# A step of a hybrid decoder: TensorE's work in the attention takes the order of the program text

## The chip, the core and the metric

The kernel runs on one core of a Trainium2 chip. A core has five engines that run side by side: TensorE (matrix products, PE in the rows), VectorE (DVE), ScalarE (ACT), GpSimd (POOL) and SyncE (SP), which here issues most transfers. Each takes its own list of instructions in the order in which it stands in the program and waits on semaphores for the others. The metric is the device time of one execution in microseconds (us); the kernel before takes 1497.58 us (median of 3 runs, 1497.58 to 1500.13).

## The reference

One step of a small decoder: a state-space layer (S5) and then an attention layer, for a prompt of 1024 tokens and for 8 samples of 8 new tokens, which have 2048 past tokens each in a paged cache. Both layers have their own weights; keys and values come once, from the stream after the S5 layer. The change touches only the attention, whose weights are "stick-breaking":

```
z = q·k * scale + bias                       # per head, strictly causal mask
log_fail = where(mask, log_sigmoid(-z), 0)
later = reverse_cumsum(log_fail) - log_fail  # all keys between this one and the query
A = where(mask, exp(log_sigmoid(z) + later), 0)
o = A @ v
x + rms_norm((o * silu(g)) @ w_out, g_post)  # g: the gate, the second half of h @ w_in
```

There are 16 heads of 64 columns, so 8 head pairs. Samples run the same on 16 pages of 128 past keys and on their own new ones.

## The kernel before, in words

The attention's main loop (in `attention`, `for slot in range(-LAG, n_row)`) runs over 128 rows. A row is one head with one block of 128 queries; pairs of heads follow each other, in a pair four groups of 256 queries (qp = 0 to 3, with growing numbers of keys), in a group two heads with two blocks each. The tiles psb, psa, psqk and psmm are PSUM banks (3, 2, 2 and 1 of them).

Three kinds of work for TensorE are woven together in the text of a slot:

- The prompt. `prompt.scores` of the row three slots ahead (LAG = 3): products psqk<-ks,qh and psqk<-ks,ql (L1139, L1140); then ScalarE forms two sigmoids (F, S; L1141, L1142), VectorE scans F (L1146, L1148), VectorE or GpSimd multiplies S by F (L1149). `prompt.turn` of the row itself: S is transposed in 128-column blocks (psb<-cst,S, L1164) and taken out masked (L1168). After each fourth row `prompt.values` of the group before: psb<-at,vr (L1182), 64 columns of the array, the two heads of the pair side by side, and then og (L1186). Keys of a pair are cut in a high and a low part (ks, L1103 on ScalarE and L1104 on VectorE); its values stand in one buffer, vr (L1107, `bufs=1`), filled again for each pair.
- The gates: `gate(ct)`, 72 full-array products per pair (psmm<-x,whi_g and wlo_g, L147 to L149) in nine pieces.
- The samples: `stream(...)`, a generator of steps: two pages of keys (kp, L990) for scores, two pages of values (vp, L949), transposes (L1004). L990 and L949 use 32 columns of the array, four instructions for its four quarters after each other. Pages come through three buffers.

`pump(slot, part)` is called twice in a slot and gives the gates and samples so many pieces that they end evenly over the pairs.

The text so written is not the order in which an engine's instructions stand. The program is built with a planner (`schedule_with_timeline_sim=True`): it goes through the instructions with a model of their durations and puts on each engine what it thinks ready first, the text's order only deciding between those that are ready. So a score product, a transpose or a piece of a gate can stand between the four quarters of a page group, or between the two heads of a value product. At run time TensorE keeps to the order that the planner wrote.

Of the kernel before, what the change touches and what calls it, by code (L numbers as in the profile page):

```python
# [144 lines left out]
def mm3(nc, ps, sh, sl, mh, ml, k, n):  # L145

    nc.tensor.matmul(ps, sh, mh, start=(k == 0), stop=False)  # L147
    nc.tensor.matmul(ps, sh, ml, start=False, stop=False)  # L148
    nc.tensor.matmul(ps, sl, mh, start=False, stop=(k == n - 1))  # L149


def kernel_body(tc, io, upto=9):
    nc = tc.nc
    with ExitStack() as root:
# [34 lines left out]
        with tc.tile_pool(name="w", bufs=2, reuse_waits="tile") as wp:  # L189
# [5 lines left out]
            with tc.tile_pool(name="y2s", bufs=1, side="right", reuse_waits="tile") as ysp:  # L195
                y2, ys = s5_glu(tc, nc, io, wp, x1, ysp, bank, zs_d, s2, *parts)
                (x1h, x1l), wq0 = s5_out(tc, nc, io, wp, x1, bank, ident, y2, ys, ysp, x1_d, gw, gains)
        attention(tc, nc, io, bank, left, gws, gw, gains, ident, x1h, x1l, wq0, x1_d, q_d, o_d)


# [405 lines left out]
def attention(tc, nc, io, bank, x1s, gws, gw, gains, ident, x1h, x1l, wq0, x1_d, q_d, o_d):  # L606
    V, Q = nc.vector, nc.gpsimd
    with ExitStack() as st:
# [146 lines left out]
        def pump(slot, part):  # L755

            pi, r = divmod(slot, 16)
            frac = (pi + sum(SHARE[: r // 4]) + SHARE[r // 4] * ((r % 4) + part) / 4) / (KT - 1)
            for f in fills:
                while f[2] < min(1.0, frac) * f[1]:  # L760
                    next(f[0], None)
                    f[2] += 1
# [3 lines left out]
        def out_steps():  # L766
            for qp in range(3, -1, -1):
                while qp not in done:
                    yield
                for t in (2 * qp, 2 * qp + 1):  # L770
                    yield from first_half(t)

        for slot in range(-LAG, n_row):
            if slot + LAG < n_row:
                prompt.scores(*rows[slot + LAG])
            if slot < 0:
                for _ in range(9 // LAG + 1):
                    next(g0, None)
                continue
            def beside(part):  # L780
                if fin is None:
                    pump(slot, part)
                else:
                    for _ in range(2):
                        next(outs, None)

            beside(0.5)
            if slot % 4 == 0 and slot:
                pi, qp = groups[slot // 4 - 1]
                prompt.values(pi, qp, sgt[pi], None if pi < KT - 1 else fin)  # L790
                if fin and pi == KT - 1:
                    done.append(qp)
            if slot == n_row - 16:
                for f in fills:
                    for _ in f[0]:
                        pass
                sst.close()
                gws.close()
                x1s.close()
                fp = st.enter_context(tc.tile_pool(name="fin", bufs=1, side="right", reuse_waits="tile"))  # L800
                fin = [[fp.tile([128, SEQ], F32R, name=f"o{n}{k}") for k in range(KT)] for n in "hl"]
                fr = st.enter_context(tc.tile_pool(name="fin_r", bufs=1, side="right", reuse_waits="tile"))
                osg = fr.tile([128, KT, NTS], F32, name="osg")
                V.tensor_tensor(osg, osam.rearrange("p k s t -> p k (s t)"), sgs, op=ALU.mult)
                ps_s = [bank("a")]
                halves = [out_half(nc, fr, io["b_wout"], 0, osg, ps_s[0])]
                for k in range(KT - 1):
                    r = fr.tile([128, SEQ], F32, name=f"or{k}", tag="or", bufs=2)
                    nc.sync.dma_start(r, o_d[k])
                    nc.scalar.activation(fin[0][k], r, AF.Copy)  # L810
                    (V if k % 2 else Q).tensor_tensor(fin[1][k], r, fin[0][k], op=ALU.subtract)

                gp = []

                def gain(pool):
                    g = pool.tile([128, 512], F32, name=f"gpost_b{len(gp)}", bufs=1)
                    nc.sync.dma_start(g, io["b_gpost"][:, len(gp) * 512 : len(gp) * 512 + 512].to_broadcast([128, 512]))
                    gp.append(g)

                gain(fr)  # L820

                def gained(name, half, src, o, acc, n=128):

                    sq = fr.tile([128, 512], F32, name=f"sqo{half}_{name}", tag="wro", bufs=2)
                    nc.scalar.activation(sq[:n], src, AF.Square, accum_out=acc[:n])
                    V.tensor_tensor(o[:n], src, gp[half][:n], op=ALU.mult)

                def out_tile(t, half, o, acc):
                    ps = bank(next(free))
                    sl = slice(t * 128, t * 128 + 128)  # L830
                    wh, wl = halves[half]
                    for k in range(KT):
                        mm3(nc, ps, fin[0][k][:, sl], fin[1][k][:, sl], wh[k], wl[k], k, KT)
                        yield
                    gained(t, half, ps, o, acc)

                def out_sample(half, o, acc):
                    f = fr.tile([128, 512], F32, name=f"osum{half}", tag="wro", bufs=2)
                    nc.scalar.activation(f[:NTS], ps_s[half][NTS:], AF.Copy)
                    V.tensor_tensor(f[:NTS], ps_s[half][:NTS], f[:NTS], op=ALU.add)  # L840
                    gained("s", half, f[:NTS], o, acc, NTS)

                first = {}
                free = chain(("mm", "a", "a") * 2, cycle(("b", "qk", "a", "b", "mm", "qk", "a", "b")))

                def firsts(t):
                    s2 = fr.tile([128, 2], F32, name=f"s2_{t}", bufs=1)
                    f = fr.tile([128, 512], F32, name=f"oa{t}", bufs=1)
                    first[t] = f, s2
                    return f, s2[:, 0:1]  # L850

                def first_half(t):
                    yield from out_tile(t, 0, *firsts(t))

                f, acc = firsts(8)
                V.memset(first[8][1], 512.0)
                out_sample(0, f, acc)
                outs = out_steps()

            prompt.turn(*rows[slot])  # L860
            beside(1)
# [37 lines left out]
def out_half(nc, pool, src, half, osg, ps, bufs=2):  # L899


    wh, wl = [], []
    for k in range(KT):
        raw = pool.tile([128, 512], F32, name=f"wr_o{half}{k}", tag="wro", bufs=bufs)
        nc.sync.dma_start(raw, src[k * 128 : (k + 1) * 128, half * 512 : half * 512 + 512])
        rows = slice(k % 2 * NTS, k % 2 * NTS + NTS)
        nc.tensor.matmul(ps[rows], osg[:, k], raw, start=(k < 2), stop=(k > 5))
        h = pool.tile([128, 512], F32R, name=f"woh{half}{k}", bufs=1)
        l = pool.tile([128, 512], F32R, name=f"wol{half}{k}", bufs=1)
        nc.scalar.activation(h, raw, AF.Copy)  # L910
        nc.vector.tensor_tensor(l, raw, h, op=ALU.subtract)
        wh.append(h)
        wl.append(l)
    return wh, wl
# [485 lines left out]
```

## Time and profile before

| | |
|---|---|
| median of 3 runs | 1497.58 us |
| profiled execution, its own time | 1500.17 us |
| its span | 1498.4 us |
| TensorE busy | 1415.8 us (94%) |
| VectorE busy | 935.0 us (62%) |
| ScalarE, GpSimd busy | 718.2 us (48%), 493.7 us (33%) |
| attention loop, in the trace | 872 to 1430 us |

Shares over the whole span mix the S5 stages with the attention, which has other limits. A matrix product's end is modelled, and products overlap in the array: so the start of one to the start of the next tells its cost, not the duration beside it. In the trace each instruction of L949, L990, L961 and L1182 stands as two records (two passes of a 32-bit product), every other product of the loop as one.

### The profile page before, as it was taken

Reading aid. Unit: us, or ns where it says so; the run is one execution under the profiler, and the core shown is the slowest. Engines: PE = TensorE matmul, PEld = TensorE weight load, DVE = VectorE, ACT = ScalarE, POOL = GpSimd, SP = SyncE. Lnnn points to the kernel's source line nnn. Section 1 sums busy time; section 2 is a strip of 40 time slices with the busy share of each in tenths; the row PEclk is TensorE's granted clock in tenths of the full one; section 3 lists DMA queues with packets and bytes.
Section 4 is the critical chain, followed back from the end, with each engine's and each line's share of the span. In section 5 each row is a group of like instructions: output and inputs, shape, how many; then the busy total and the mean of one; then the engine's idle time right before and its main releaser. Section 6 shows DMA issues by size and latency. Waiting matters only on the chain.

```text
span 1498.4 us, 26819 instructions
## 1 busy us (share of the span) xinstructions
PE 1415.8 (94%) x9648; PEld 1145.8 (76%) x9648; DVE 935.0 (62%) x1506; ACT 718.2 (48%) x1424; POOL 493.7 (33%) x473
## 2 busy tenths in 40 slices
PE   4987988899999989999999999999998999998997
PEld 3987978899977889999988877666565665565766
DVE  6877887758755531110122149897888888789545
ACT  5233454454434433332333347676665766576321
POOL 6556565325412132222111012433323233334200
PEclk9999999999999999999999999999999999999999
DMA  5345556674134252232288755979878686754026
GB/s 197 103 129 139 140 126 163 145 251 145 58 106 132 91 224 91 85 123 100 103 314 298 255 201 192 339 284 326 295 257 289 250 308 219 268 190 139 11 82 213
DMA packets 129670, 276.41 MB, mean 184 GB/s; under 512 B 21633, under 2 KB 66562, under 8 KB 129538
## 3 DMA queue, kind: packets, MB, share of 16 engines
q1 hardware_dynamic: 127234, 268.41, 54.0%
q10 hardware_dynamic: 2304, 6.29, 1.3%
q8 instruction: 76, 1.25, 0.3%
q14 instruction: 56, 0.46, 0.1%
HBM read 224.55 MB, written 39.35 MB: 176 GB/s over the span
## 4 chain that ended last, share of the span: by engine, by line
PE 75%; DVE 9%; POOL 5%; DMA 4%; issue 3%; ACT 2%; SPq 1%; DVEq 0%; POOLq 0%; ACTq 0%
PE psmm L147 7%; PE psmm L149 7%; PE psmm L148 7%; PE psqk L147 6%; PE psqk L148 6%; PE psqk L149 6%; PE psa L949 5%; PE psb L1182 5%; PE psb L1164 4%; PE psa L990 4%; PE psqk L1139 3%; PE psqk L1140 2%; DMA cf<-cs 2%; PE psa L147 2%; PE psa L149 2%
## 5 line engine op out<-in xcount | busy, mean ns | idle before, releaser
L1120 POOL TENSOR_TENSOR ql<-q,qh 128x256 fp32r<-128x256 f32 x64 | 62.5, 977 | 285.6 <-ACT qh L1119 246.5
L1141 ACT ACTIVATE F<-psqk,bp 128x384 f32<-128x384 f32 (+2 forms) x192 | 111.3, 580 | 64.6 <-PE psqk L1140 49.2
L1146 DVE TENSOR_TENSOR_SCAN F<-F,maskb 128x256 f32<-128x256 f32 (+3 forms) x128 | 131.2, 1030 | 14.0 <-ACT F L1141 13.6
L1149 POOL TENSOR_TENSOR S<-S,F 128x255 f32<-128x255 f32 (+3 forms) x64 | 100.8, 1574 | 115.7 <-DVE F L1148 22.5
L1142 ACT ACTIVATE S<-psqk,bp 128x384 f32<-128x384 f32 (+2 forms) x192 | 111.4, 583 | 22.7 <-PE psb L1164 22.6
L1164 PE MATMUL psb<-cst,S 128*128 128x128 f32 x576 | 96.7, 285 | 4.4 <-DVE og L1186 3.8
L1164 PEld LDWEIGHTS psb<-cst,S 128*128 128x128 f32 x576 | 67.3, 143 | 35.1 <-issue 20.5
L1148 DVE TENSOR_TENSOR_SCAN F<-F 128x384 f32<-128x384 f32 (+1 forms) x64 | 78.9, 1233 | 20.4 <-ACT F L1141 19.8
L1182 PE MATMUL psb<-at,vr 128*64 128x256 f32 (+1 forms) x640 | 90.0, 369 | 1.2 <-DVE at L1168 1.2
L949 PE MATMUL psa<-vp,sat 128*32 128x256 f32 x1024 | 86.1, 388 | 0.1
L1139 PE MATMUL psqk<-ks,qh 128*128 128x384 f32 (+2 forms) x192 | 77.4, 404 | 6.9 <-DVE ks L1104 5.2
L990 PE MATMUL psa<-kp,qbd 128*32 128x256 f32 x1024 | 75.5, 389 | 0.5 <-PE psb L1164 0.5
L1182 PEld LDWEIGHTS psb<-at,vr 128*64 128x64 f32 x640 | 46.7, 137 | 36.6 <-issue 10.3
L1168 DVE TENSOR_TENSOR at<-psb,maskb 128x384 f32<-128x384 f32 (+3 forms) x128 | 60.3, 478 | 21.3 <-PE psb L1164 20.7
L147 PE MATMUL psmm<-xh,whi_u 128*128 128x408 f32 (+1 forms) x192 | 65.3, 341 | 3.7 <-ACT ut L278 3.1
L147 PE MATMUL psmm<-x,whi_g 128*128 128x408 f32 (+1 forms) x192 | 66.6, 347 | 1.1 <-DVE gt L739 1.1
L943 DVE TENSOR_TENSOR_SCAN sF<-sF 128x513 f32<-128x513 f32 x32 | 44.4, 1388 | 36.1 <-ACT sF L940 35.8
L1139 PEld LDWEIGHTS psqk<-ks,qh 128*128 128x128 f32 x192 | 37.0, 193 | 37.8 <-ACT S L1142 12.8
L1140 PE MATMUL psqk<-ks,ql 128*128 128x384 f32 (+2 forms) x192 | 65.8, 344 | 0.0
L148 PE MATMUL psmm<-xl,whi_u 128*128 128x408 f32 (+1 forms) x192 | 65.4, 341 | 0.0
L149 PE MATMUL psmm<-x,wlo_g 128*128 128x408 f32 (+1 forms) x192 | 64.9, 338 | 0.2 <-DVE wlo_g L141 0.2
L148 PE MATMUL psmm<-x,whi_g 128*128 128x408 f32 (+1 forms) x192 | 65.1, 339 | 0.0
(452 smaller groups left out, 4234.6 us busy)
## 6 DMA issues: line engine op xcount, KB each, us to landing
kp<-cache_kT SPq DMA_DIRECT2D x128, 512.0 KB, 6.0
vp<-cache_v SPq DMA_DIRECT2D x128, 512.0 KB, 5.7
cf<-cs SPq DMA_DIRECT2D x32, 256.0 KB, 5.4
q<-q_d SPq DMA_DIRECT2D x128, 64.0 KB, 4.6
u_d<-ut SPq DMA_DIRECT2D x8, 544.0 KB, 2.8
ug<-u_d SPq DMA_DIRECT2D x64, 68.0 KB, 2.9
y_d<-gt SPq DMA_DIRECT2D x64, 68.0 KB, 2.4
zs_d<-zt SPq DMA_DIRECT2D x8, 544.0 KB, 4.5
```

The lines of the kernel that those rows point to most:

```text
L147: nc.tensor.matmul(ps, sh, mh, start=(k == 0), stop=False)
L148: nc.tensor.matmul(ps, sh, ml, start=False, stop=False)
L149: nc.tensor.matmul(ps, sl, mh, start=False, stop=(k == n - 1))
L949: self.nc.tensor.matmul(po[32 * r : 32 * r + 32, 0:256], a[:, 32 * r : 32 * r + 32], rhs[:, r * 256 : (r + 1) * 256], start=start, stop=stop)
L990: nc.tensor.matmul(ps[32 * r : 32 * r + 32, half * 256 : half * 256 + 256], self.qbd[:, 2 * r + e, s, :], kt[:, :, 2 * r + e, :], start=(e ...
L1139: nc.tensor.matmul(ps[:, :m], qh[:, w], ks[:, c0 : c0 + m], start=True, stop=False)
L1141: nc.scalar.activation(F[:, c0 : c0 + m], ps[:, :m], AF.Sigmoid, bias=bp[:, 1, h : h + 1], scale=-0.125)
L1142: nc.scalar.activation(S[:, c0 : c0 + m], ps[:, :m], AF.Sigmoid, bias=bp[:, 0, h : h + 1], scale=0.125)
L1146: V.tensor_tensor_scan(fr, fr, self.maskb[:, 512 - m : 512][:, ::-1], 1.0, ALU.mult, ALU.max)
L1149: (Q if i % 2 else V).tensor_tensor(S[:, 0 : n - 1], S[:, 0 : n - 1], F[:, 1:n], op=ALU.mult)
L1164: nc.tensor.transpose(ps[:, j * 128 : (j + 1) * 128], S[:, (j0 + j) * 128 : (j0 + j + 1) * 128], self.ident)
L1182: nc.tensor.matmul(po[hs, o:256], self.vr[pi][:, j, hs], ats[hh][j // 4][:, j % 4, o:256], start=(j == 0), stop=(j == nj - 1))
```

## The change

The loop runs within a context that tells the planner to leave TensorE in the order of the text; it ends where the last gates and samples have been written (the slot 16 rows before the end). The other engines are planned as before, now around a TensorE whose order is given. No instruction is added, dropped or changed. The new lines move the numbers of the lines behind them by 3 or 4: L1182 is L1186 after, L949 is L953, L990 is L994, L1164 is L1168, L1107 is L1111.

```
+        fixed = st.enter_context(ExitStack())
+        fixed.enter_context(tc.manual_schedule(engines={mybir.EngineType.PE}))
         for slot in range(-LAG, n_row):
             if slot + LAG < n_row:
                 prompt.scores(*rows[slot + LAG])
...
                 for f in fills:
                     for _ in f[0]:
                         pass
+                fixed.close()
                 sst.close()
```

Three places show what moves. The first is on TensorE, at the last value products of the third pair (psb524, heads at4 and at5, values vr2) and a page group of a sample (psa509<-vp4_2_1, eight instructions, two groups of four). Before:

```order
L1182 MATMUL psb524_12025<-at4_3_0_11666,vr2_10696 64x256
L949 MATMUL psa509_11689<-vp4_2_1_11996,sat4_2_11754 32x256 x4
L1004 MATMUL psa522_11961<-cst_63,sS4_1_11898 128x128 x4
L1182 MATMUL psb524_12025<-at5_3_0_11846,vr2_10696 64x256
L1182 MATMUL psb524_12025<-at4_3_0_11666,vr2_10696 64x256
L1182 MATMUL psb524_12025<-at5_3_0_11846,vr2_10696 64x256
L1182 MATMUL psb524_12025<-at4_3_0_11666,vr2_10696 64x256
L1182 MATMUL psb524_12025<-at5_3_0_11846,vr2_10696 64x256
L1182 MATMUL psb524_12025<-at4_3_0_11666,vr2_10696 64x256
L949 MATMUL psa509_11689<-vp4_2_1_11996,sat4_2_11754 32x256 x4
L1182 MATMUL psb524_12025<-at5_3_0_11846,vr2_10696 64x256
```

The same instructions after, the first ten of the sixteen value products:

```order
L953 MATMUL psa509_11691<-vp4_2_1_11998,sat4_2_11756 32x256 x8
L1186 MATMUL psb524_12027<-at4_3_0_11668,vr2_10698 64x256
L1186 MATMUL psb524_12027<-at5_3_0_11848,vr2_10698 64x256
L1186 MATMUL psb524_12027<-at4_3_0_11668,vr2_10698 64x256
L1186 MATMUL psb524_12027<-at5_3_0_11848,vr2_10698 64x256
L1186 MATMUL psb524_12027<-at4_3_0_11668,vr2_10698 64x256
L1186 MATMUL psb524_12027<-at5_3_0_11848,vr2_10698 64x256
L1186 MATMUL psb524_12027<-at4_3_0_11668,vr2_10698 64x256
L1186 MATMUL psb524_12027<-at5_3_0_11848,vr2_10698 64x256
L1186 MATMUL psb524_12027<-at4_3_1_11669,vr2_10698 64x256
L1186 MATMUL psb524_12027<-at5_3_1_11849,vr2_10698 64x256
```

The value products stood in three runs, of one, six and nine, with page groups and a sample's transposes between them; they now stand in one run of sixteen, behind the whole page group.

The second place is the next value page of the same sample (vp4_1_0), 30 instructions on. On TensorE before:

```order
L949 MATMUL psa509_11689<-vp4_1_0_12223,sat4_1_11966 32x256 x2
L1139 MATMUL psqk533_12170<-ks7_11728,qh7_1_12115 128x512
L1140 MATMUL psqk533_12170<-ks7_11728,ql7_1_12116 128x512
L949 MATMUL psa509_11689<-vp4_1_0_12223,sat4_1_11966 32x256 x2
L148 MATMUL psmm534_12177<-x11_0_4561,whi_g4_11991 128x408
L149 MATMUL psmm534_12177<-x10_0_4559,wlo_g4_11992 128x408
L949 MATMUL psa509_11689<-vp4_1_0_12223,sat4_1_11966 32x256 x4
```

After:

```order
L1143 MATMUL psqk538_12218<-ks6_11727,qh6_2_12206 128x384
L1144 MATMUL psqk538_12218<-ks6_11727,ql6_2_12207 128x384
L953 MATMUL psa509_11691<-vp4_1_0_12225,sat4_1_11968 32x256 x8
L1168 MATMUL psb539_12254<-cst_63,S6_3_12072 128x128 x4
L1143 MATMUL psqk540_12262<-ks6_11727,qh6_2_12206 128x256
```

A group of four was cut in two halves by score products, and a gate's products stood between the groups; now both groups stand on end.

The third is SyncE's queue where the values of the fourth pair (vr3) are asked for. Before:

```order
L929 DMA vp4_1_0_12223<-cache_v 128x1024
L1116 DMA q2_7_2_12295<-q_d_71 64x256
L1107 DMA vr3_11731<-o_v 128x8x128
L1116 DMA q2_7_2_12295<-q_d_71 64x256
L1188 DMA o_d_72<-og2_3_12042 128x256
```

After:

```order
L1120 DMA q2_7_2_12297<-q_d_71 64x256
L932 TENSOR_LOAD pt_5326
L932 ISA x2
L932 TENSOR_LOAD pt_5326
L932 ISA x2
L932 TENSOR_LOAD pt_5326
L932 ISA x2
L1111 DMA vr3_11733<-o_v 128x8x128
L1192 DMA o_d_72<-og2_3_12044 128x256
L932 TENSOR_LOAD pt_5326
L932 ISA x2
L1102 DMA kr4_12726<-o_kT 128x1024
```

The request for vr3 stands behind the same page and query loads, but now the key load of the next pair (kr4) comes close behind; at the pairs whose values are vr1, vr2, vr5 and vr6 the key load stands right ahead of it.

## Rows read from the trace of the kernel before

**Rows 1.** The page's first line.

```profile
span 1498.4 us, 26819 instructions
```

**Rows 2.** Busy time by stage, attention: stage, length, engines, clock, DMA share, GB/s.

```profile
core 0: us, PE busy (x) PEld busy (x) DVE busy (x) ACT busy (x) POOL busy (x), PEclk, DMA share, GB/s
900.00:1000.00 100.00, 99.53 (x869) 67.18 (x868) 93.69 (x132) 71.33 (x142) 34.72 (x26) 1.00 0.76 267
...
922.00:972.00 50.00, 50.00 (x471) 32.60 (x471) 45.39 (x63) 33.56 (x67) 20.44 (x16) 1.00 0.94 330
...
948.70:1348.20 399.50, 391.20 (x3236) 247.34 (x3235) 336.00 (x471) 263.91 (x521) 133.56 (x105) 0.99 0.78 273
```

**Rows 3.** TensorE's waits, 872 to 1430 us: total us, times, longest.

```profile
PE psqk L1139 <- DVE ks L1104: 5.2, 2, 3.6
PE psb L1164 <- DVE og L1186: 3.8, 1, 3.8
```

**Rows 4.** TensorE in time, gate products: start, duration, engine, line, tiles, forms.

```profile
884.80 0.35 PE L149 MATMUL psmm<-x,wlo_g 128*128 128x408 f32 x1
884.99 0.35 PE L147 MATMUL psmm<-x,whi_g 128*128 128x408 f32 x1
```

**Rows 5.** TensorE in time, page products (L949), cut and whole groups.

```profile
1086.75 0.63 PE L949 MATMUL psa<-vp,sat 128*32 128x256 f32 x4
1087.31 0.50 PE L1139 MATMUL psqk<-ks,qh 128*128 128x512 f32 x1
...
1088.53 0.45 PE L148 MATMUL psmm<-x,whi_g 128*128 128x408 f32 x1
1088.82 0.35 PE L149 MATMUL psmm<-x,wlo_g 128*128 128x408 f32 x1
1089.10 0.64 PE L949 MATMUL psa<-vp,sat 128*32 128x256 f32 x8
1089.67 0.39 PE L1139 MATMUL psqk<-ks,qh 128*128 128x256 f32 x1
...
1093.36 1.07 PE L949 MATMUL psa<-vp,sat 128*32 128x256 f32 x16
1094.36 0.55 PE L1164 MATMUL psb<-cst,S 128*128 128x128 f32 x3
```

**Rows 6.** TensorE in time, the third pair's last value products (L1182).

```profile
1073.57 0.65 PE L1182 MATMUL psb<-at,vr 128*64 128x256 f32 x2
1074.14 0.64 PE L949 MATMUL psa<-vp,sat 128*32 128x256 f32 x8
...
1075.30 1.52 PE L1182 MATMUL psb<-at,vr 128*64 128x256 f32 x12
1076.75 0.64 PE L949 MATMUL psa<-vp,sat 128*32 128x256 f32 x8
1077.32 2.16 PE L1182 MATMUL psb<-at,vr 128*64 128x256 f32 x18
1079.40 0.33 PE L1164 MATMUL psb<-cst,S 128*128 128x128 f32 x1
```

**Rows 7.** The values' transfer: SyncE's request, the first use, landing of the seven.

```profile
1013.73 0.40 SPq L1107 DMA_DIRECT2D vr<-o_v  x1
...
1024.24 0.87 PE L1182 MATMUL psb<-at,vr 128*64 128x256 f32 x8
...
DMA to landing us min/median/max: 4.2/6.6/8.1
```

**Rows 8.** TensorE after its longest wait, and the clock there by stage.

```profile
1137.80 0.44 PE L1139 MATMUL psqk<-ks,qh 128*128 128x128 f32 x1 [3.61 <-DVE ks L1104]
...
1137.00:1141.00 4.00, 3.20 (x22) 1.84 (x23) 2.71 (x5) 0.82 (x3) 1.88 (x2) 0.50 1.00 373
1141.00:1144.00 3.00, 3.00 (x18) 1.70 (x20) 0.89 (x2) 1.35 (x4) 0.00 (x0) 0.65 1.03 330
```

More of the change, by code (lines that the diff above doesn't have):

```diff
@@ L771, in out_steps @@
                     yield from first_half(t)
+        fixed = st.enter_context(ExitStack())
+        fixed.enter_context(tc.manual_schedule(engines={mybir.EngineType.PE}))
         for slot in range(-LAG, n_row):
@@ L796, in attention @@
                         pass
+                fixed.close()
                 sst.close()
```

## The prediction, on record before the changed kernel ran

> **What bounds the kernel now.** I read the profile in four steps. First the busy time by stage: the change touches only the attention, from 872 to 1430 us of a span of 1498.4 us [rows 1], and in it I looked at the six head pairs between the last value product of the first pair (948.7 us) and that of the seventh (1348.2 us). There TensorE is busy 391.2 of 399.5 us, VectorE 336.0, and the transfers hold 0.78 of the DMA engines [rows 2]. Second, who TensorE waits for: eleven kinds of wait, the two longest 5.2 and 3.8 us in all [rows 3]. So TensorE sets the pace there, and the reader is to see that taking waits away can bring little. Third, because a busy TensorE is not one at its peak, I read the starts of its instructions in time. Fourth, what a forced order can make late: the one value buffer and its transfer [rows 7], and the clock after a wait [rows 8].
>
> **The starts tell what an order costs.** Full-array products of the gate follow each other every 0.19 us [rows 4]. The page products (L949, L990) use 32 columns of the array, four of them side by side. A whole group of four, eight records, takes 1089.10 to 1089.67, so 0.57 us; two groups on end take 1093.36 to 1094.36, so 1.00 us: 0.43 us for a group and 0.14 us for a run of them. Half a group, four records, takes 0.56 us (1086.75 to 1087.31): 0.42 without the run's 0.14, as much as a whole one [rows 5]. So a part of a group costs what the group costs. A run of L1182 (64 columns, two side by side) takes 0.57 us with one instruction and 1.45 us with six [rows 6]. Written as run plus columns, with a lone one counting as two because its two passes have no partner, 4 steps are 0.88 us: 0.22 us for a step and 0.13 us for a run. The third run there, nine instructions of which two are half as wide, should then take 0.13 + 8 x 0.22 + 2 x 0.11 = 2.11 us; the rows give 2.08. Last, each crossing between full array and columns: the product before the columns takes 0.28 us instead of 0.19 (1088.82 to 1089.10), the one after them 0.29 (1088.53 to 1088.82) [rows 4, 5]: 0.09 us each.
>
> [...]
>
> **The change part by part.** No instruction is added or removed; TensorE's order in the loop is that of the text, and the other engines' orders shift by some places with it. I counted runs along both orders, from the first score product to the end of the last value products and a little behind.
> - Runs of L949 and L990: 154 before, 101 after: 53 x 0.14 = 7.4 us.
> - Groups of four cut in parts: 63 runs with a part before, none after. A half costs 0.42 where its share of 0.43 is 0.215, so 0.21 us too much; a quarter loses more, three quarters less, so 0.21 stands for all: 63 x 0.21 = 13.2 us.
> - Runs of L1182: 72 before, 38 after: 34 x 0.13 = 4.4 us. Runs of odd length: 52 before, 8 after: 44 x 0.22 = 9.7 us.
> - Crossings: 400 before, 248 after: 152 x 0.09 = 13.7 us.
> - The small L961 (13 runs, then 10) I leave at nothing: under 1 us.
> The sum is 48 us less of TensorE's own time, and by the same count nearly all of it lies in the six pairs; in the first and the last pair the two orders differ by about 3 us, one each way. From both sides: none of it comes through if TensorE waits instead, all of it if it does not.
>
> What hides it: VectorE. Its 336.0 us in the six pairs are the same work after. 399.5 - 48 = 351.5 us would ask for 96% of it. Its highest share in a stretch of 100 us of this attention is 93.69% [rows 2]; at that share the six pairs take 336.0/0.937 = 359 us, 41 us less than now; at 92% 365 us, 34 us less. I take 38. Here the in-order engine matters: the transposes of a row stand three rows behind its scores, and if VectorE's scan of it is late, everything behind waits, gates and pages too, which could have run.
>
> A wait that the change adds: there is one value buffer. The next pair's values (vr) are asked for when the last product of the old pair has read it, and needed by the first value product of the new pair. Before, a request at 1013.73 is needed at 1024.24, after 10.5 us; landing takes 4.2, 6.6 and 8.1 us (least, median, most) [rows 7]. By the prices above, TensorE has after the change 4.9 to 6.7 us of work between the two places, some 6 us. With 0.3 us to the request, a median landing leaves it 0.9 us short, the longest 2.4; for seven pairs 6 us, 17 at most, nothing if the landing is short. Queued behind it are the scores and transposes of the new pair's first rows and a page group; the page group's buffer, and so a page's transfer, waits with them. VectorE catches up in such a wait, so it is not all on top: I take 6 us.
>
> In sum: 38 - 6 = 32 us faster. Against its own time, 1500.17 us for the profiled execution, that is 1468; this execution is 2.6 us above the median of the runs shown, 1497.58, so I predict **1466 us**.
>
> **The rivals.**
> - Vector-bound in lockstep. VectorE's work is not even over a pair: it has two key subtractions and many short rows at the start of a pair, TensorE its longest rows at the end. If three rows of lead do not level that, each stage takes the longer of the two, and VectorE's 84% (336.0 of 399.5) hardly rises: at 86% the six pairs take 391 us, with the 6 us of waits about as long as now; at 88%, 382 us, 12 us faster with the waits. I give it 3 to 12 us faster, 1490 us. For it: TensorE's waits now are mostly for VectorE [rows 3]. Against it: 93.69% over 100 us with 99.53 us of TensorE beside it [rows 2].
> - Slower: the value transfer, and the clock. SyncE's queue is in order; if the request for vr stands behind a query load or a key load that waits, it goes out 4 to 5 us late, and TensorE waits some 5.5 us at each of seven boundaries instead of 1. [...] 7 x (4.5 + 3) = 52 us against the 32: 1518 us. The forecast's 32 us are 4.6 us per boundary; with 3 us of clock, 1.6 us more of wait than its 1 us use them up, so it decides from a wait of some 2.6 us per pair, if the clock falls each time. For it: in the new order a key load can stand right beside vr. Against: with all its waits, the clock over the six pairs is 0.99 now [rows 2]. [...]
> - No change within 0.2% (3 us, about what a measurement of this kernel can tell): the cut groups cost nothing because they fill time in which TensorE would have waited. Against: between 922 and 972 us it is busy 50.00 of 50 us with cut groups throughout [rows 2], so nothing is there to fill.
> - More than forecast: VectorE reaches 96% and the waits of before go too, 48 us and some 8 of waits: 1442 us. For it only that the planner of before could not see the real landings; against it VectorE's share.
>
> **How the numbers follow.** Forecast 0.64, its own range 12 to 52 us faster, 1446 to 1486. Lockstep 0.12, slower 0.11, no change 0.05, more 0.08. Faster by over 0.2% is 0.64 + 0.12 + 0.08 = 0.84, within it 0.05, slower 0.11. The range runs from 1444 (all of TensorE's 48 us and a few of waits) to 1497 (lockstep and most of no change); outside lie the slower rival and most of the fastest one, under 2 in 10.
>
> **What would show it.** The starts: value products in runs of 4, 8, 12 and 16 at 0.22 us a step, page groups at 0.57 or 1.00 us, no part of a group. TensorE's busy time in the attention down by some 45 us or its waits up by what is missing; VectorE at 90% or more in the six pairs, and a pair in 60 to 61 us where it is 66.6 now. New waits for VectorE's scans and, once a pair, at the first value product for vr. Wrong if the six pairs keep their 399.5 us with VectorE at 84%, or if the clock falls at every pair.

## The result: 2.8% slower, where 2.1% faster was forecast

The changed kernel takes 1541.11 us (median of 4 runs, 1536.10 to 1544.64), the kernel before in the same session 1498.86: a ratio of 1.0279, 95% interval 1.0246 to 1.0312. The forecast was 1466, its range ended at 1497. I read the profile after in the order of the prediction. First the page, its first line and the totals of the two engines that the forecast set against each other (busy us, share of the span, instructions; against [rows 1] and the 1415.8 and 935.0 us of before):

```profile
span 1542.9 us, 26814 instructions
...
PE 1402.7 (91%) x9648; PEld 1154.0 (75%) x9648; DVE 942.0 (61%) x1506; ACT 721.3 (47%) x1424; POOL 489.1 (32%) x473
```

TensorE works 13.1 us less in a span that is 44.5 us longer. Second the stages. The last value product of the first pair has moved from 948.7 to 971.9 us, that of the seventh from 1348.2 to 1394.9; so 23.2 us are lost up to the end of the first pair, 23.5 in the six pairs, and 2.2 come back behind them. Busy time by stage of the changed kernel: 25 us early in the first pair, and the six pairs (columns as in [rows 2]):

```profile
875.00:900.00 25.00, 21.48 (x182) 18.09 (x174) 9.52 (x30) 7.10 (x19) 1.49 (x3) 0.86 0.47 166
...
971.90:1394.90 423.00, 366.73 (x3149) 246.31 (x3147) 354.41 (x466) 264.47 (x515) 127.89 (x107) 0.97 0.70 242
```

And the same 25 us of the kernel before:

```profile
875.00:900.00 25.00, 22.33 (x163) 18.43 (x156) 17.29 (x38) 14.08 (x35) 7.24 (x8) 1.00 0.47 170
```

In the six pairs TensorE is busy 24.5 us less than in [rows 2] (366.73 against 391.20) and idle 48.0 us more (56.3 against 8.3): 23.5 us. VectorE is busy 84% (354.41 of 423.00), as before, and not 90% or more. In the first pair VectorE has 9.52 us of work in a stretch where it had 17.29: it is starved while rows are short. By the starts of TensorE's instructions the idle time there is 15.2 us against 3.0; the granted clock is 0.50 for some 10 us, in which gate products follow each other every 0.34 us (884.07 to 886.45) and not every 0.18 (887.25 to 888.35); and 64 records of page products (eight groups, 3.4 us at 0.43 each) and 16 of the small L965, some 0.4 us, are done before the pair ends that were done later. With the lost half of those 10 us, 5, that is 21 us; another 1.8 is that the first score product starts later in the span (873.63 us against 871.85). Together that is 22.8 of the 23.2 us.

Third, who TensorE waits for in the six pairs of the changed kernel (total us, times, longest; against [rows 3]):

```profile
PE psqk L1143 <- ACT S L1146: 38.6, 45, 2.6
PE psmm L147 <- DVE gt L739: 6.1, 4, 2.5
PE psb L1186 <- DMA vr<-o_v: 3.5, 4, 1.9
PE psa L1008 <- DVE sF L943: 2.8, 3, 1.6
```

The first row is 38.6 of the 56.3 idle us. The kernel before had 0.4 us of this kind in its six pairs:

```profile
PE psqk L1139 <- ACT S L1142: 0.4, 1, 0.4
```

Not VectorE holds TensorE here but ScalarE's second sigmoid of a row, S. The wait is larger than that row. TensorE loads the weights of a product ahead of it (PEld: the load for the L1144 product of 1126.99 us starts at 1126.87, while that of L1143, begun at 1126.79, runs), and in the changed kernel the loads for the score products wait for S too (before: 10.6 us, 13 times):

```profile
PEld psqk L1143 <- ACT S L1146: 64.1, 96, 2.9
```

These waits overlap the products' own (at 1127.81 us 0.75 for the load and 0.54 for the product end together), so the two rows are not to be added; the experiments show what they cost together. Fourth, then, what ScalarE and VectorE wait for in the same stretch:

```profile
ACT S L1146 <- PE psb L1168: 36.8, 25, 3.4
ACT gt L738 <- DVE gt L739: 28.1, 15, 3.9
...
DVE F L1150 <- ACT F L1145: 28.0, 28, 3.2
```

So TensorE waits for S on ScalarE, and S waits for TensorE's transposes (L1168): a ring. The same rows of the kernel before, in its six pairs:

```profile
ACT S L1142 <- PE psb L1164: 15.6, 16, 2.4
...
DVE F L1148 <- ACT F L1141: 19.8, 20, 2.5
...
DVE F L1146 <- ACT F L1141: 9.1, 12, 1.7
```

S waited less than half as long for the transposes. VectorE's two scans together waited 28.9 us for F, as long as the 28.0 after: that wait did not grow, it only moved to the masked scan.

A place of it in the changed kernel's time line (start, duration, engine, line, tiles; in brackets the idle time before it and what ended it):

```profile
1125.68 0.87 PE L1186 MATMUL psb<-at,vr 128*64 128x256 f32 x8 [0.85 <-DMA vr<-o_v]
...
1126.49 0.55 PE L1168 MATMUL psb<-cst,S 128*128 128x128 f32 x3
...
1127.07 0.69 ACT L1146 ACTIVATE S<-psqk,bp 128x512 f32<-128x512 f32 x1 [1.72 <-PE psb L1168]
...
1127.81 0.45 PE L1143 MATMUL psqk<-ks,qh 128*128 128x384 f32 x1 [0.54 <-ACT S L1146]
...
1129.36 0.66 PE L1168 MATMUL psb<-cst,S 128*128 128x128 f32 x4
...
1130.06 0.95 ACT L1146 ACTIVATE S<-psqk,bp 128x256 f32<-128x256 f32 x2 [1.01 <-PE psb L1168]
...
1130.59 0.39 PE L1143 MATMUL psqk<-ks,qh 128*128 128x256 f32 x1 [0.56 <-ACT S L1146]
```

The text explains it. S has three buffers, and the text of slot s calls the scores of row s+3 first, then gates and samples, then the transposes of row s. S of row s+3 goes into the buffer of row s, so ScalarE may not write it until those transposes are done; in the text's order they stand behind the scores, the first of the slot's two portions of gates and samples and, in every fourth slot, the value products. Until S has read it, a psqk bank stays taken, and there are two; so the next score products wait, and all of TensorE's list behind them. ScalarE takes its list in order too (in the trace its 1366 activations start in the order of the program): with S waiting at its head, the next F cannot start either. In the rows: the value products start after 0.85 us of waiting for vr, the transposes come late, S has waited 1.72 us for them, and the next score product 0.54 us for S; the same again 2.8 us on.

### The profile page after: what moved, and what is told of

It is laid out like the page before. It is cut to its first block, busy times and chain, and to the rows that moved or that the text cites. A ratio compares the mean times of both kernels' runs of the same rounds, so it can differ in the third digit from the quotient of the medians.

```text
span 1542.9 us, 26814 instructions
## 1 busy us (share of the span) xinstructions
PE 1402.7 (91%) x9648; PEld 1154.0 (75%) x9648; DVE 942.0 (61%) x1506; ACT 721.3 (47%) x1424; POOL 489.1 (32%) x473
## 3 DMA queue, kind: packets, MB, share of 16 engines
q1 hardware_dynamic: 127234, 268.41, 52.9%
## 4 chain that ended last, share of the span: by engine, by line
PE 60%; DVE 15%; DMA 7%; ACT 6%; POOL 5%; issue 5%; SPq 2%; DVEq 0%; POOLq 0%; ACTq 0%
PE psqk L147 6%; PE psqk L148 6%; PE psmm L147 6%; PE psqk L149 6%; PE psmm L149 5%; PE psmm L148 5%; PE psa L953 3%; PE psb L1186 3%; DVE F L1150 3%; PE psa L994 3%; DMA cf<-cs 2%; PE psqk L1143 2%; DVE F L1152 2%; PE psb L1168 2%; DMA vr<-o_v 2%
## 5 line engine op out<-in xcount | busy, mean ns | idle before, releaser
L1150 DVE TENSOR_TENSOR_SCAN F<-F,maskb 128x256 f32<-128x256 f32 (+3 forms) x128 | 147.6, 1153 | 49.9 <-ACT F L1145 49.4
L1153 POOL TENSOR_TENSOR S<-S,F 128x255 f32<-128x255 f32 (+3 forms) x64 | 93.7, 1464 | 172.8 <-ACT S L1146 89.2
L1143 PE MATMUL psqk<-ks,qh 128*128 128x384 f32 (+2 forms) x192 | 83.0, 434 | 47.6 <-ACT S L1146 47.1
L1146 ACT ACTIVATE S<-psqk,bp 128x384 f32<-128x384 f32 (+2 forms) x192 | 105.1, 583 | 40.1 <-PE psb L1168 39.7
L1143 PEld LDWEIGHTS psqk<-ks,qh 128*128 128x128 f32 x192 | 37.7, 196 | 87.4 <-ACT S L1146 79.0
L1168 PE MATMUL psb<-cst,S 128*128 128x128 f32 x576 | 90.3, 284 | 2.9 <-DVE og L1190 2.5
L1168 PEld LDWEIGHTS psb<-cst,S 128*128 128x128 f32 x576 | 66.0, 143 | 31.1 <-issue 19.0
L1186 PE MATMUL psb<-at,vr 128*64 128x256 f32 (+1 forms) x640 | 72.7, 363 | 4.0 <-DMA vr<-o_v 3.5
L147 PE MATMUL psmm<-x,whi_g 128*128 128x408 f32 (+1 forms) x192 | 68.4, 356 | 8.2 <-DVE gt L739 8.2
L953 PE MATMUL psa<-vp,sat 128*32 128x256 f32 x1024 | 71.5, 396 | 1.5 <-DMA vp<-cache_v 1.5
L1186 PEld LDWEIGHTS psb<-at,vr 128*64 128x64 f32 x640 | 44.4, 137 | 34.9 <-issue 8.2
L1172 DVE TENSOR_TENSOR at<-psb,maskb 128x384 f32<-128x384 f32 (+3 forms) x128 | 60.5, 476 | 16.3 <-PE psb L1168 15.8
L994 PE MATMUL psa<-kp,qbd 128*32 128x256 f32 x1024 | 69.6, 392 | 0.8 <-DMA kp<-cache_kT 0.8
L1144 PE MATMUL psqk<-ks,ql 128*128 128x384 f32 (+2 forms) x192 | 67.7, 353 | 0.0
L147 PE MATMUL psmm<-xh,whi_z 128*128 128x408 f32 (+1 forms) x192 | 66.0, 344 | 0.0
L149 PE MATMUL psmm<-xh,wlo_z 128*128 128x408 f32 (+1 forms) x192 | 65.8, 343 | 0.0
L148 PE MATMUL psmm<-xl,whi_z 128*128 128x408 f32 (+1 forms) x192 | 65.8, 343 | 0.0
```

Source lines behind the costliest of these rows:

```text
L953: self.nc.tensor.matmul(po[32 * r : 32 * r + 32, 0:256], a[:, 32 * r : 32 * r + 32], rhs[:, r * 256 : (r + 1) * 256], start=start, stop=stop)
L994: nc.tensor.matmul(ps[32 * r : 32 * r + 32, half * 256 : half * 256 + 256], self.qbd[:, 2 * r + e, s, :], kt[:, :, 2 * r + e, :], start=(e ...
L1143: nc.tensor.matmul(ps[:, :m], qh[:, w], ks[:, c0 : c0 + m], start=True, stop=False)
L1146: nc.scalar.activation(S[:, c0 : c0 + m], ps[:, :m], AF.Sigmoid, bias=bp[:, 0, h : h + 1], scale=0.125)
L1150: V.tensor_tensor_scan(fr, fr, self.maskb[:, 512 - m : 512][:, ::-1], 1.0, ALU.mult, ALU.max)
L1168: nc.tensor.transpose(ps[:, j * 128 : (j + 1) * 128], S[:, (j0 + j) * 128 : (j0 + j + 1) * 128], self.ident)
```

## The experiments

My theory after this reading: TensorE's own time did fall by about what was forecast; the text's order closes rings through short buffers and through the other engines' lists, and each stops TensorE whole, first the ring of S. (The edits move the line numbers by 1 to 5: L1168 of the change is L1169 in e1 and L1172 in e8.) The rivals: the score banks alone are too few; the loss is in the first rows and what leads into them; the prices of the runs were wrong and nothing was there to gain.

**e1 and e2: the transposes first.** The same move in the changed kernel and in the kernel before:

```
         for slot in range(-LAG, n_row):
+            if slot >= 0:
+                prompt.turn(*rows[slot])
             if slot + LAG < n_row:
                 prompt.scores(*rows[slot + LAG])
...
-            prompt.turn(*rows[slot])
             beside(1)
```

> The changed kernel with one line moved: in each slot the transposes of the row (prompt.turn) come before the scores of the row three further on, not at the end of the slot. Theory A (score buffer ring): there are three buffers S, the row three further on wants the one that the row itself still holds until it is transposed, and in the text's order its scores stand ahead of those transposes; ScalarE's second sigmoid then waits for the transposes, holds the score banks, and TensorE waits for a bank. Expects ScalarE's wait for the transposes (39.7 us in the changed kernel) under 10 us, TensorE's wait for ScalarE's S (47.1 us) under 15 us, and 1455 to 1485 us. Theory B (VectorE and TensorE in lockstep, the lead of three rows is too small): the lead gets a little shorter still, so 1535 to 1560 us with as much waiting.

> The kernel before with the same line moved and the planner's order kept. Theory A: the planner takes what is ready, so the place in the text matters little: 1480 to 1510 us. Theory B says the same. If this gains as much as the move does under the fixed order, the move helps by itself and does not show the ring.

e1: 1525.7 us, 1.0181 (1.0162 to 1.0200) of the kernel before; so 15.4 us of the 42 are gone, a time between those of the two theories. e2: 1494.7 us, 0.9974 (0.9960 to 0.9988): with the planner the move is worth some 4 us, so most of e1's gain is not the move by itself. In e1 the six pairs take 405.9 us (busy time by stage):

```profile
968.10:1374.00 405.90, 354.60 (x3155) 250.65 (x3153) 354.99 (x470) 258.35 (x518) 125.48 (x106) 0.95 0.73 253
```

The waits of theory A are gone there: TensorE's products wait 1.9 us for S (its weight loads 4.6), and S no longer waits for transposes at all. Other waits stand in their place; the last row is ScalarE's longest:

```profile
PE psa L1009 <- DVE sF L944: 11.4, 6, 3.5
PE psmm L147 <- DVE gt L739: 8.1, 7, 2.8
PE psb L1169 <- DVE at L1173: 8.0, 6, 2.3
...
ACT gt L738 <- DVE gt L739: 42.8, 18, 5.4
```

What follows: the ring is real and costs about 15 us net; taking it away lets the next waits through. TensorE is busy 12.1 us less than in the change, for the same products to within six records and at a lower granted clock (0.95 against 0.97), and still idle 51.3 us. So a part of the ring's wait had most likely stood in the change as busy time.

**e3: two rows of lead.** The changed kernel with the scores two slots ahead, so that S of row s+2 never needs the buffer of row s:

```
-LAG = 3
+LAG = 2
```

> The changed kernel with LAG = 2: scores are written two rows ahead of the transposes, so the buffer S that they want has been free since the slot before; the lead is a row shorter. Theory A: ScalarE's wait for the transposes falls under 10 us and the kernel gets faster than 1541, some 1470 to 1510 us (the shorter lead costs some of it). Theory B (lead too small): slower than 1541, 1560 us or more.

1525.06 us, 1.0166 (1.0149 to 1.0183): the same gain as e1, reached from the other side, and again between the two theories. S does not wait for transposes here either, and TensorE is busy 351.28 us in the six pairs, 15.4 less than in the change. Its longest wait in the six pairs is for a sample's scan:

```profile
PE psa L1008 <- DVE sF L943: 19.7, 8, 6.0
PE psmm L147 <- DVE gt L739: 10.9, 4, 6.6
```

**e4: three score banks.** The rival that two psqk banks are too few; the third is taken from psb:

```
-        bank.use({"mm": 1, "qk": 2, "a": 2, "b": 3})
+        bank.use({"mm": 1, "qk": 3, "a": 2, "b": 2})
```

> The changed kernel with three PSUM banks for scores instead of two and two instead of three for transposes and value products. Theory A: the ring stays, ScalarE still waits for the transposes (about 40 us); TensorE's wait for a score bank falls by a part, since one more piece of scores fits: 1515 to 1545 us. Theory C (too few score banks as such): the wait for ScalarE's S goes from 47 to under 15 us and the kernel comes to 1490 us or less.

1556.23 us, 1.0378 (1.0361 to 1.0396), slower than the change and outside both ranges. In the six pairs the wait for S falls to less than half, and a longer one comes with the missing psb bank:

```profile
PE psb L1168 <- DVE og L1190: 31.0, 14, 3.3
PE psqk L1143 <- ACT S L1146: 16.6, 27, 2.3
```

So the score banks are not the cause: S itself waits for the transposes as theory A said, 54.8 us in these pairs against 36.8 in the change. The price of the third bank, the missing psb bank, hides what it gains. A fourth S buffer, the direct test, wasn't tried.

**e5: the planner orders the lead.** The fixed order begins at slot 0 and not three slots earlier:

```
-        fixed.enter_context(tc.manual_schedule(engines={mybir.EngineType.PE}))
         for slot in range(-LAG, n_row):
+            if slot == 0:
+                fixed.enter_context(tc.manual_schedule(engines={mybir.EngineType.PE}))
```

> The changed kernel with the fixed order begun at slot 0, so that the lead-in (the first gate's 72 products and the scores of the first three rows) is left to the planner. Theory A (lead-in): in the changed kernel the first pair takes 98.3 us against 76.9 before, since the text puts the whole first gate ahead of the second row's scores and VectorE stands idle (8.1 of 25 us busy from 872, before 15.6); with the planner there the first pair takes 77 to 84 us and the kernel 1518 to 1528 us. Theory B (VectorE is the bound and catches up later): the pairs behind get longer by the same, and the time stays within 5 us of 1541.

1540.28 us, 1.0266 (1.0246 to 1.0287), as the change; its first pair takes 97.9 us from its first score product (98.3 in the change, 76.9 before). Theory B's time came, and the three lead slots are not where the first pair loses.

**e6: the gate's two pieces.** A gate piece is two sigmoids on ScalarE, each followed by a product on VectorE. In ScalarE's list the second sigmoid waits for the first product. On top of e1, both sigmoids come first:

```
-                for o, src in (
+                pieces = (
...
+                for o, src in pieces:
                     nc.scalar.activation(o, src, AF.Sigmoid)
+                for o, src in pieces:
                     V.tensor_tensor(o, src, o, op=ALU.mult)
```

> The kernel of the first experiment (transposes first) with the gate's evacuation written in another order: both sigmoids of a part on ScalarE, then both products on VectorE, where it was sigmoid, product, sigmoid, product. Theory A (ScalarE is held by VectorE's queue: 50.7 us of waits for the gate's first product there): that wait falls under 15 us, the scores are taken out sooner, 1495 to 1515 us. Theory B (VectorE itself is the bound): the wait goes, the time stays, 1520 to 1530 us.

1514.52 us, 1.0095 (1.0078 to 1.0112), as theory A had it: 11 us less than e1, 13 by the ratios. ScalarE's 42.8 us of e1 for the gate's product are gone; its longest waits in the six pairs are now for TensorE, and TensorE's longest is for a sample's scan:

```profile
ACT F L1148 <- PE psqk L1147: 42.2, 23, 4.4
ACT at L1177 <- PE psb L1171: 41.1, 26, 4.0
...
PE psa L1011 <- DVE sF L946: 18.4, 8, 4.5
```

**e7: a sample's transposes one step later,** on top of e1, so that its scan has time while the second pages' products run:

```
-            x.turn(c)
-            yield
             if prev:
                 prev[0].values(prev[1], 1)
                 yield
+            x.turn(c)
+            yield
```

> The kernel of the first experiment with the samples' transposes one step later in their stream (behind the second page of values, not between the two). Theory A (each piece that the text puts too close behind its VectorE work stops TensorE): its waits at these transposes (24.5 us together in the first experiment) fall under 8 us, 1505 to 1517 us. Theory B: VectorE is late everywhere, the wait turns up at another place, 1520 to 1530 us.

1523.55 us, 1.0159 (1.0138 to 1.0180): within the intervals no different from e1, as theory B had it. Its waits over the attention show why: TensorE waits 4.1 us for the sample's scan where it waited 15.4 in e1, and 23.9 us for the gate where it waited 11.2:

```profile
PE psmm L147 <- DVE gt L739: 23.9, 15, 3.6
PE psb L1169 <- DVE at L1173: 11.3, 8, 2.7
...
PE psa L1009 <- DVE sF L944: 4.1, 2, 3.6
```

**e8: all three edits, with e5's start.**

> The first experiment with the planned lead-in, the gate's pieces and the later sample transposes together. Theory A (the text's places are the cause, one by one): the gains add to 45 us or more, 1465 to 1490 us, faster than the kernel before. Theory B (VectorE in lockstep): 1500 to 1520 us, VectorE at 90% or more in the six pairs.

1509.75 us, 1.0064 (1.0047 to 1.0081). Three quarters of the loss are mended, and the six pairs take 395.0 us, 4.5 less than before [rows 2]. TensorE is busy 351.27 us of them and idle 43.7, in waits of many kinds, none over 10 us in all. The gains did not add up as theory A said; the time is theory B's, with VectorE at 89% of the six pairs, just short of its 90%. Whether VectorE is what holds them is asked by e11. Busy time by stage, first the start of the attention, then the six pairs:

```profile
878.00:938.00 60.00, 51.30 (x436) 37.64 (x438) 48.99 (x75) 37.13 (x80) 17.61 (x16) 0.94 0.57 197
...
967.00:1362.00 395.00, 351.27 (x3154) 246.69 (x3152) 349.78 (x471) 258.58 (x517) 130.50 (x106) 0.97 0.74 257
```

And TensorE's longest waits in the six pairs of e8:

```profile
PE psmm L147 <- DVE gt L741: 9.4, 7, 2.9
PE psb L1172 <- DVE at L1176: 8.2, 5, 3.6
PE psa L998 <- ACT sat L1014: 5.7, 4, 3.4
PE psa L957 <- DMA vp<-cache_v: 4.5, 6, 2.0
PE psb L1190 <- DMA vr<-o_v: 3.4, 4, 1.7
```

**e9: the text's order from the second pair on.** e8, with `if slot == 16` in place of `if slot == 0`.

> All three edits of the run before, but the planner orders TensorE through the first head pair as well and the text's order begins with the second pair (slot 16). In that run the first pair takes 98.1 us where the kernel before has 76.9; TensorE stands idle there 16 us against 3, at steps that depend on one another and stand close together while the rows are short (gate after gate product, a sample's transposes after its scan, its last sums), the clock is at half for 13.6 us, and some 5 us are page work that the kernel before does later. Theory A: that idle time and its clock are the fixed order's own, so 12 to 17 us go: 1493 to 1498 us, level with the kernel before or 0.4% faster, TensorE idle under 5 us up to the end of the first pair. Rival B: the first pair is long because of the edits or of what the transfers do there, not because of the order: it stays within 3 us of 1510.

1506.83 us, 1.0037 (1.0023 to 1.0051), 3 us below e8 and not 12 to 17; the two intervals overlap. By the time alone this is rival B to within 0.2 us. The rows tell another story (busy time by stage; the first line is to be held against e8's first above, the last is the six pairs):

```profile
878.00:938.00 60.00, 57.42 (x487) 41.58 (x489) 52.16 (x86) 40.03 (x87) 18.55 (x16) 1.00 0.60 217
938.00:964.40 26.40, 19.53 (x172) 12.37 (x172) 16.84 (x24) 10.88 (x23) 8.80 (x8) 0.81 0.72 254
964.40:1358.20 393.80, 348.16 (x3154) 243.46 (x3152) 349.29 (x464) 258.45 (x517) 131.52 (x105) 0.98 0.74 260
```

With the planner TensorE works 57.42 of these 60 us, against 51.30 in the text's order: the idle time of the first rows was the order's own. Then the seam: in the next 26.4 us, to the end of the first pair, it is idle 6.9 and its clock is 0.81. Two waits are 6.2 of the 6.9: 4.0 us for a sample's scan product and 2.2 for the cut of the next pair's keys. My reading, which no run tested, is that the planner at the seam has nothing more to bring forward; the expectation had left that out. The next run settles rival B: with the same edits and the planner throughout, the first pair takes 81.0 us, against 92.6 here and 98.1 in e8.

**e10: the three edits under the planner.** The kernel before with the edits of e1, e6 and e7, and no fixed order.

> The kernel before (the planner orders TensorE throughout) with the edits of the text that mended the other: transposes of a row first in its slot, both gate sigmoids ahead of the products, a sample's transposes one step later. Theory A: the kernel before lost nothing to these places, since the planner moved other work in: TensorE is busy 391 of 399.5 us in the six pairs and only some 8 us are to be had, 1490 to 1496 us. Rival B: the edits are good by themselves, and the text's order is worth less than nothing even when mended: 1480 us or less, below the run with the order from the second pair on.

1483.85 us, 0.9883 (0.9868 to 0.9898): the best version, 1.2% faster than the kernel before, better than the first theory and short of the rival's 1480. The six pairs (busy time by stage):

```profile
950.20:1337.00 386.80, 378.13 (x3191) 244.31 (x3190) 343.69 (x472) 259.93 (x519) 135.96 (x106) 1.00 0.79 274
```

Against e9, which has the same edits and the text's order in these pairs (TensorE busy 348.16 of 393.80), this is the change taken by itself, in a kernel with the three edits: the text's order saves TensorE 30 us of busy time, at a granted clock of 0.98 against 1.00, and costs it 37 us of idle (45.6 against 8.7). Of the 15.5 us by which e10's span is shorter than that of the kernel before, 12.7 lie in the six pairs, where TensorE is busy 13.1 us less. Some 5 of these can be the clock, which stood at 0.50 for 10 us of these pairs before and never in e10, and 2 to 3 are page groups done earlier (45 records fewer). How the gain divides over the edits was not measured beyond e2's 4 us.

**e11 and e12: less for VectorE.** The product of S and F is left out for the even rows, in e8 and in the kernel before.

```
-        (Q if i % 2 else V).tensor_tensor(S[:, 0 : n - 1], S[:, 0 : n - 1], F[:, 1:n], op=ALU.mult)
+        if i % 2:
+            Q.tensor_tensor(S[:, 0 : n - 1], S[:, 0 : n - 1], F[:, 1:n], op=ALU.mult)
```

> The three edits with the text's order, and the product of S and F for the even rows left out (VectorE, 35.3 us in the six pairs of the kernel before), so that the samples' work and the transposes come on time. It computes something else. Theory A: TensorE's own time is shorter by the 48 us of the forecast, and VectorE with the chain through it holds it back: with 35 us less of VectorE the six pairs fall from 395 to 355 to 370 us, 1470 to 1485 us in all, and TensorE's busy share in them rises from 0.89 to over 0.93. Rival B: the prices of the runs are wrong, TensorE has no time to give back: the six pairs stay over 385 us, 1500 us or more.

> The kernel before with the same product left out for the even rows: the control. It computes something else. Theory A: TensorE, busy 391.2 of 399.5 us in the six pairs, bounds the kernel before, so 35 us less of VectorE give at most the 8 us of waits: 1490 to 1498 us. Rival B: the kernel before waits for VectorE as well and TensorE's busy time only stretches over it: 1480 us or less.

e11: 1491.27 us, 0.9938 (0.9922 to 0.9953); e12: 1489.24 us, 0.9924 (0.9908 to 0.9939). e12 ends 0.8 us below theory A's range and far from rival B's. The six pairs of e11 take 382.7 us, between its two theories, and those of e12 392.2 (busy time by stage, e11 and then e12):

```profile
959.40:1342.10 382.70, 345.08 (x3157) 243.82 (x3153) 313.15 (x424) 257.09 (x517) 127.97 (x106) 0.98 0.77 267
```

```profile
953.00:1345.20 392.20, 388.09 (x3236) 247.49 (x3234) 312.27 (x428) 262.79 (x522) 124.56 (x106) 1.00 0.79 278
```

TensorE's longest waits in e11's:

```profile
PE psa L957 <- DMA vp<-cache_v: 8.9, 8, 1.6
PE psb L1191 <- DMA vr<-o_v: 6.9, 3, 2.6
PE psmm L147 <- DVE gt L741: 6.7, 6, 2.4
PE psa L998 <- ACT sat L1014: 5.4, 4, 3.4
```

Two things follow. TensorE's own time: 345.08 against 388.09 us, 43.0 less, of which 3 to 4 are page groups that e11 has done earlier (79 records fewer in the stretch). Over the whole span, where the work is the same, 1371.5 against 1413.9: 42.4 us less. Its mean clock is the lower one, 0.980 against 0.985; if every moment of the lower level fell on work, another 7.4 us would be the clock's (1487.5 x 0.020 - 1487.7 x 0.015). So 42 to 50 us: the prices of the runs were right together; no run tests one of them alone. And VectorE is not alone in holding the rest: with 36.6 us less work for it than in e8 (349.78 to 313.15) the six pairs lose only 12.3, VectorE is at 82%, and TensorE is still idle 37.6 us, for pages, for vr, for gates and for a sample's copies in turn.

## Why the prediction was wrong, point by point

- **TensorE bounds the kernel before** [rows 2, 3]: right. e12 takes 23.7 us of VectorE's work in the six pairs away (336.00 to 312.27) and gains 12 us in all, some more than the 8 us that its expectation allowed; the six pairs give 7.3 of them, and TensorE's idle time there is 4.1 us. But busy is not unhindered: the next points show how much of that time the planner had filled.
- **The sum of 48 us** [rows 4 to 6]: right in size as a whole; its terms were not tested one by one. By the starts from 860 to 1480 us, the change has 104 runs of page products where there were 155, none cut in a group where 63 were, 38 runs of value products for 72, and 265 crossings for 426 (here a change between page and value products counts too). A group now takes what rows 5 say: in the changed kernel 16 records start at 1093.24 and the next product at 1094.24. e11 against e12 gives 42 to 50 us. In the changed kernel itself 13.1 us of it show as busy time, and by its mean clock (0.977 against 0.982 over the span) some 8 us more. Most of the rest is the ring again, in score products and weight loads that wait: in e1 and e3, which open it, TensorE is busy 12 to 15 us less. As an estimate, with each moment of the lower clock taken off at half, TensorE's busy time in the six pairs is 386 us in the kernel before and in e12, 355 in the change, and 336 to 340 in e1, e3, e8, e9 and e11; some 4 of the difference are page groups done earlier.
- **What hides it is VectorE, "I take 38":** this is the step that failed. It took VectorE's share, 93.69% over its best 100 us, as the only thing that can hide TensorE's saving, and put TensorE's wait for S at nothing. In its place the runs showed a ring through the three S buffers: the idle time came from what waits for what. e1 and e3 open the ring and take back 15 to 16 us each; behind it stand the gate's pieces (e6, 11 us) and small waits that no edit removed, so that even with three edits the order stays slower. Nor were VectorE's 336.0 us "the same work after": they became 354.41 (the last section says by what). The prediction saw the danger for one case, a scan that comes late for the transposes. It did not follow S: three buffers, LAG = 3, scores of s+3 ahead of the transposes of s in the text. That was to be read from the code and the order. With the planner's order S cost TensorE's products 0.4 us; with the text's, 38.6.
- **"A wait that the change adds", vr, 6 us** [rows 7]: the mechanism was right, the term about twice too large: 3.5 us in four waits. But it was the only wait that was priced, where the text's order takes away, at every wait of TensorE, the work that the planner had moved into it. The gate's second sigmoid (11 us, e6), the samples' transposes (by themselves nothing, e7) and the short rows of the first pair (23.2 us with the work that moved there) stood in the same text.
- **Lockstep** was the nearest rival: VectorE stayed at 84%, as it said. It ended at 3 to 12 us faster, since it let TensorE wait for the longer of two stages but not in a ring. **The slower rival** had the right sign by another way: its vr wait is small, and the clock fell elsewhere. The 3 us of clock at a boundary in its sum are the loss of [rows 8] (0.50 for 4 us and 0.65 for 3), seen behind one wait of the kernel before. In the changed kernel the granted clock went from 0.99 to 0.97 in the six pairs, where none of its six falls comes within 19 us behind a pair's first value product, and from 1.00 to 0.86 between 875 and 900 us. TensorE's waits in the six pairs are mostly for ScalarE, 38.6 us, and the granted clock is lower all the same. **No change** argued that cut groups fill time in which TensorE would have waited. I set against it that TensorE was busy 50.00 of 50 us; but that is what a filled wait looks like. e9 against e10 shows what was true in it: 30 us are saved, so the cut groups did cost, and 37 us of waits are laid open, so they did fill.
- **The chances:** 0.11 for slower was too little for a change that takes the choice away on the engine that is 98% busy, when only one of its waits had been followed through.

## What to carry to other kernels

An engine that a planner keeps busy can be busy because work was moved into its waits, as here; before its order is fixed, list every buffer with its count, and ask for each whether the instruction that frees it stands behind one that needs it, through the in-order lists of the other engines too. Costs that a planner's order has on the engine itself (cut groups, crossings) can be real and still be the cheaper side: here 30 us of busy time against 37 of idle, e9 against e10. The three edits of the text that the fixed order asked for (to free before filling, not to interleave two engines within a helper, to put a product further behind the scan that it needs) were worth 1.2% together under the planner.

## What the runs showed of the hardware

VectorE's time for the same work depends on what GpSimd does beside it: 0.67 to 2.23 us for a sample's product (L948) in the changed kernel. Its row by line (least, median and longest in ns, first and last start):

```profile
L948 DVE TENSOR_TENSOR sS<-sS,sF x32: 673/693/2235, 748.2 to 1369.7; 128x512 f32<-128x512 f32 x32
```

The longest, in the time line:

```profile
1010.78 2.67 POOL L1153 TENSOR_TENSOR S<-S,F 128x1023 f32<-128x1023 f32 x1 [2.89 <-ACT S L1146]
...
1011.76 2.23 DVE L948 TENSOR_TENSOR sS<-sS,sF 128x512 f32<-128x512 f32 x1
```

GpSimd's product ends at 1013.45, VectorE's 0.54 us later, at 1013.99. All 32 rows of the changed kernel fall in the same pattern. Ten began while a GpSimd operation was running; they took 0.73 to 2.23 us, and every one ended 0.55 us after it, to within 0.01. Six in which a GpSimd operation began later, and 16 with none beside them, took 0.67 to 0.69 us. The kernel before shows it too: ten of its 32 (L944 there) began behind a GpSimd operation, took 0.88 to 2.31 us and ended 0.55 us after it, to within 0.01; the other 22 took 0.67 to 0.70. So VectorE is not slowed in proportion; by these rows most of its work, 0.55 of 0.69 us, comes after GpSimd's end.

This also tells what became of VectorE's time. Taken against the median of its own kind and shape without a GpSimd operation ahead, the operations that began behind one lost 37.9 us in the six pairs of the kernel before and 52.9 in those of the change: 15.0 of the 18.4 us by which VectorE is busy longer. The masked scans, 97.7 us for 94 before and 114.7 for 96 after, are the largest part. No run was made to change it.
